# The group norm of an RWKV-7 branch: squares, sums of squares and final scaling by ScalarE's activations with bias and scale per partition

## The chip, the core and the metric

The kernel runs on one core of a Trainium2 chip. Its engines are TensorE (PE in the profile, its weight loads PEld), VectorE (DVE), ScalarE (ACT), GpSimd (POOL) and SyncE (SP), which issues nearly all DMAs. The metric is the device time of one execution in microseconds (us), lower is better.

## The reference, cut to what matters

One layer of a streaming encoder is computed for a prompt of 2048 tokens and for 8 running streams of 16 tokens each. A combined projection feeds three mixers, RWKV-7, Mamba-2 and stick-breaking attention, whose outputs go through one output projection. The part that matters here is the end of the RWKV-7 mixer, a norm over the 64 values of each head and token:

```python
def rwkv7_branch(ua, gate, S0, shift0, p):
    ...
    S_T, y = lax.scan(step, S0.astype(f32), seq)
    y = y.swapaxes(0, 1)
    mean = jnp.mean(y, axis=-1, keepdims=True)
    var = jnp.mean(jnp.square(y - mean), axis=-1, keepdims=True)
    y = (y - mean) * lax.rsqrt(var + GN_EPS) * p['rwkv_ln_w']... + p['rwkv_ln_b']...
    y = y + jnp.sum(r * k * p['rwkv_r_k'].astype(f32), axis=-1, keepdims=True) * v
    out = y.reshape(B, T, D_A) * jax.nn.silu(gate.astype(f32))
```

## The kernel before

The tokens are cut into four groups: 512 prompt tokens and all 128 sample tokens, then three times 512 prompt tokens. A group is cut into units of 256 prompt tokens, and group 0 has one more of the 128 sample tokens. The twelve RWKV heads are handled in six pairs, so that the 128 partitions hold two heads. For each pair and unit `stage_rwkv` runs `rwkv_dense` (projections of k, r, v and the gate g), `rwkv_prep` (decays, masks, products), `rwkv_inv` and `rwkv_inv2` (inverse of a triangular matrix), `rwkv_chain` (the recurrence over chunks of 64 tokens, the pass spoken of below) and `rwkv_out` (the group norm, the transpose back to channels by PE, bias, gate, and the store to the scratch tensor `oT`). The output of a unit is put off: `rwkv_out` of one unit stands in the program behind the pass of the next unit, and behind the filler work of its own step. The filler work is a list of pieces of the other mixers and of the output projection of the previous group (`fill`), spread over the twelve steps of a group.

After the RWKV and Mamba-2 stages of all groups (up to about 3060 us) comes attention with the rest of the output projection.

No instruction is issued in the order of the program text. All calls on the engines are recorded by `Plan`, which at `emit` orders them with a list scheduler: it keeps an estimate of each instruction's cost (`cost`), of the lag between engines (`LAG`) and of when a buffer comes free, and takes next the instruction that can start first; at a tie the one that stands first in the program. Every engine, SP's DMA queue too, then works through its list in that order. A tile pool's tag is a ring of buffers. Apart from two PSUM tags (`AHEAD`, pd and pg) a ring's buffers are given out strictly in the order of the program. Rings that matter here:

- `tw`: four buffers for short-lived results of all kinds (projections on their way to the token shift, the convolution, gates, squares).
- `py`: one PSUM bank, used in turn by a pass of the recurrence and by the transposed result of `rwkv_out`.
- `oo`: the output of `rwkv_out`, two buffers (one in group 0); before, the squares `ysq` too.
- `gmean`, `gvar`, `rq_m`, `rq_y`, `rq_t`: small tiles of one column per chunk, two buffers each.

In `rwkv_out` the tile `Ysb` holds a unit's y with tokens of two chunks' heads on the partitions and `m` chunks of 64 values along the free axis: m is 4 for a unit of 256 tokens and 2 for the sample unit. `small_rsqrt` takes a root's inverse on DVE: two steps to scale and guess, then three rounds of three instructions. `tw(n)` gives the next buffer of the ring, `py()` the bank, `sp` is the pool of small tiles. V, S, G and Y are VectorE, ScalarE, GpSimd and SP's queue. All engine calls pass through one helper, so the profile shows one line (L420) for all of them and is read by the names of tiles: `Ysb<-Ysb,gmean` is the subtraction, `ysq<-Ysb` the squares, `gvar<-ysq` their sum, `Ysb<-Ysb,rq_y` the scaling, `py<-ident,Ysb` the transposes, `oo<-py,vech` the copy with weight and bias.

Of the kernel before, what the change touches and what calls it, by code (L numbers as in the profile page):

```python
# [7 lines left out]
F32 = mybir.dt.float32  # L8
# [3 lines left out]
AF = mybir.ActivationFunctionType  # L12
ALU = mybir.AluOpType
AX = mybir.AxisListType
# [66 lines left out]
UN = 256  # L81
# [357 lines left out]
def _build(ctx, tc, nc, A, O):  # L439
    plan = Plan(tc)  # L440
    V, S, G, T, Y = (plan.engine(e, x) for e, x in zip("VSGTY", (nc.vector, nc.scalar, nc.gpsimd, nc.tensor, nc.sync)))
# [16 lines left out]
    def pg():  # L458
        return pp.tile([128, 512], F32, name="pg", tag="pg", bufs=3)
# [4 lines left out]
    def py():  # L464
        return pp.tile([128, 512], F32, name="py", tag="py", bufs=1)

    def mm(out, lhsT, rhs, start=True, stop=True):
        T.matmul(out, lhsT, rhs, start=start, stop=stop, skip_group_check=True)
# [17 lines left out]
    def trn(out, in_):  # L486
        k = in_.shape[0]
        T.transpose(out, in_, ident[0:k, 0:k])
# [22 lines left out]
    def small_rsqrt(ss, n, scale, eps, tag):  # L511

        m = sp.tile([128, n], F32, name="rq_m", tag=tag + "m")
        y = sp.tile([128, n], F32, name="rq_y", tag=tag + "y")
        t = sp.tile([128, n], F32, name="rq_t", tag=tag + "t")
        V.tensor_scalar(m, ss, scale, eps, ALU.mult, ALU.add)
        V.tensor_scalar(y.bitcast(I32), m.bitcast(I32), -0.5, 1597463007.0, ALU.mult, ALU.add)
        for _ in range(3):
            V.tensor_tensor(t, y, y, ALU.mult)
            V.scalar_tensor_tensor(t, t, -0.5, m, ALU.mult, ALU.mult)  # L520
            V.scalar_tensor_tensor(y, t, 1.5, y, ALU.add, ALU.mult)
        return y
# [11 lines left out]
    def tw(n):  # L534
        return wp.tile([128, 536], F32, name="tw", tag="tw", bufs=4)[:, 0:n]
# [91 lines left out]
    def h_scale(tiles, xs=None):  # L627

        n = len(tiles)
        ss = sp.tile([128, 2, 5], F32, name="hss", tag="hss")  # L630
        for i, (c, p0) in enumerate(tiles):
            for q in range(2):
                x = xs[i][q] if xs else xhalf(p0, q)
                S.activation(tw(512) if xs else x, x, AF.Square, accum_out=ss[:, q, i:i + 1])
        s1 = sp.tile([128, 5], F32, name="hs1", tag="hs1")
        V.tensor_tensor(s1[:, 0:n], ss[:, 0, 0:n], ss[:, 1, 0:n], ALU.add)
        r = small_rsqrt(s1[:, 0:n], n, 1.0 / D, 1e-6, "h")
        return [r[:, i:i + 1] for i in range(n)]
# [529 lines left out]
    def rwkv_out(g, u, d, gate, pr, Ysb, pool):  # L1168
        n, m = u.n, u.nch
        y3 = Ysb[:, 0:m, :]  # L1170
        mean = sp.tile([128, 6], F32, name="gmean", tag="gmean")
        V.reduce_sum(mean[:, 0:m], y3, axis=AX.X)
        V.tensor_scalar(mean[:, 0:m], mean[:, 0:m], 1.0 / 64, None, ALU.mult)
        V.tensor_tensor(y3, y3, mean[:, 0:m].unsqueeze(2).to_broadcast([128, m, 64]), ALU.subtract)
        sq = pool.tile([128, UN], F32, name="ysq", tag="oo", bufs=1 if g.s else 2)
        s3 = sq[:, 0:n].rearrange("p (c v) -> p c v", v=64)
        G.tensor_tensor(s3, y3, y3, ALU.mult)
        var = sp.tile([128, 6], F32, name="gvar", tag="gvar")
        V.reduce_sum(var[:, 0:m], s3, axis=AX.X)
        rs = small_rsqrt(var[:, 0:m], m, 1.0 / 64, 64e-5, "g")  # L1180
        V.tensor_tensor(y3, y3, rs.unsqueeze(2).to_broadcast([128, m, 64]), ALU.mult)
        p = py()
        if u.s:
            with plan.together():
                for c_ in range(m):
                    for o in (slice(0, 64), slice(64, 128)):
                        mm(p[o, 64 * c_:64 * c_ + 64], Ysb[o, c_, :], ident[o, o])
        else:
            for i in range(m // 2):
                trn(p[:, 128 * i:128 * i + 128], Ysb[:, 2 * i:2 * i + 2, :].rearrange("p h v -> p (h v)"))  # L1190

        o = pool.tile([128, UN], F32, name="oo", tag="oo", bufs=1 if g.s else 2)
        S.activation(o[:, :n], p[:, :n], AF.Identity, bias=vh(V_LNB + pr), scale=vh(V_LNW + pr))
        G.tensor_tensor(o[:, :n], o[:, :n], d["bo"], ALU.add)
        G.tensor_tensor(o[:, :n], o[:, :n], gate[:, u.c0:u.c0 + n], ALU.mult)
        for c, k, t in g.segs(u.c0, n):
            Y.dma_start(oT[pr, :, t:t + k], o[:, c - u.c0:c - u.c0 + k])
# [25 lines left out]
    def stage_rwkv(g, h, dpool, NB):  # L1223
# [39 lines left out]
        def chain(i):  # L1263
            pr, k = todo[i]
            uds = [(us[k], ds[pr][k])]
            S0T = None
            if k == 0 and smp:
                S0T = rwkv_states_in(pr, pool)
                uds = [(u, ds[pr][j]) for j, u in smp] + uds
            for u, d in uds:  # L1270
                prv = ds[pr][k - 1] if k and not u.s else None
                nxt = ds[pr][k + 1] if k + 1 < len(us) and not u.s else None
                y, Sn = rwkv_chain(u, d, pr, pool, S0T, prv, nxt)
                out()
                if "g" not in Ds[pr]:
                    dense(pr, "g")
                done.append(lambda u=u, d=d, y=y: rwkv_out(g, u, d, Ds[pr]["g"], pr, y, pool))
                if u.s:
                    rwkv_states_out(pr, Sn, pool)
# [269 lines left out]
    g = GROUPS[0]  # L1549
    early = ExitStack()  # L1550
    pool = early.enter_context(tc.tile_pool(name="m", bufs=1))
# [8 lines left out]
    rs = h_scale(g.tiles[:2], xt[:2])  # L1560
# [87 lines left out]
    p = pg()  # L1648
# [13 lines left out]
    def vh(i):  # L1662
        return vech[:, i:i + 1]
# [39 lines left out]
    p = pg()  # L1703
# [7 lines left out]
    p = pg()  # L1711
# [12 lines left out]
    for d in dD:  # L1724
        m = NCH * 8 * 2064 + 128
        for i in range(0, m, 128 * 323):
            n = min(128 * 323, m - i)
# [14 lines left out]
    with tc.tile_pool(name="r0", bufs=1) as pool:  # L1742
        rw.send((pool, fill))
        w = tw(512).rearrange("p (a c) -> p a c", c=128)
        p = pg()
# [16 lines left out]
    with tc.tile_pool(name="r", bufs=1) as pool:  # L1762
        for gi in range(1, len(GROUPS)):
            g = GROUPS[gi]
# [29 lines left out]
    with tc.tile_pool(name="fin", bufs=1) as pool:  # L1794
        r = pool.tile([64, 6, 128], F32, name="r")
        for q in range(2):
            p = pg()
# [7 lines left out]
        for q in range(2):  # L1805
            p = pg()
# [6 lines left out]
        p = pg()  # L1813
# [25 lines left out]
    p = pt()  # L1839
# [240 lines left out]
```

## Time and profile before

| | us |
|---|---|
| median of 3 runs | 3867.22 |
| lowest and highest run | 3865.18, 3870.82 |
| the profiled execution's own time | 3871.62 |
| its span (first to last instruction) | 3869.9 |
| PE busy | 3385.2 (87%) |
| DVE busy | 2746.8 (71%) |
| ACT busy | 1724.5 (45%) |
| POOL busy | 1672.4 (43%) |
| mean granted clock of TensorE | 0.933 |

A row of a group of instructions has the line, the engine, the operation, the tile written and, behind the arrow, the tiles read, the shapes, the count, then busy time in us and the mean duration of one in ns, and behind the second bar the idle time of the engine just before them with what ended it. A row of waits has the waiting engine and its tile, the engine and tile waited for, the us in total, the times and the longest. A row of a timeline has the start in us, the duration in us, and the instruction. Durations of neighbours on one engine overlap a little, so their sum can be more than the time they take.

### The profile page before, as it was taken

The numbers are of one execution on the slowest core, as the hardware profiler recorded it, in microseconds if no ns is written. First come the engines' busy times: TensorE is split into PE (matmuls) and PEld (weight loads), VectorE is DVE, ScalarE is ACT, GpSimd is POOL, SyncE is SP. The second block draws the span as 40 slices with busy tenths as digits, with TensorE's granted clock in tenths as the row PEclk, the third lists the DMA queues.
The fourth block names the chain that finished last, engine by engine and source line by source line (L and its number), as shares of the span: only waits on it lengthen the run. The fifth ranks groups of instructions, "written<-read, shape, count | busy, mean of one in ns | idle before, by whom it ended". The sixth has DMA issues, their size and how long they took to land. (4 is left out here: it accounts for less than half of the span.)

```text
span 3869.9 us, 68238 instructions
## 1 busy us (share of the span) xinstructions
PE 3385.2 (87%) x23086; PEld 2749.6 (71%) x23086; DVE 2746.8 (71%) x6621; ACT 1724.5 (45%) x4134; POOL 1672.4 (43%) x2621
## 2 busy tenths in 40 slices
PE   7988999977988898988889998888999688989998
PEld 7877888867776676776667777766777555666665
DVE  7657778876698778657886875688778553456665
ACT  4544444433454444434444443445444343445554
POOL 4544555434555655644456555445555323000000
PEclk9998999978989899999899999989999889999999
DMA  4332333335425433553254336324532587765542
GB/s 120 97 107 61 95 92 78 78 103 145 121 59 158 140 89 101 153 149 94 71 154 110 78 84 180 101 68 128 150 82 64 154 212 223 176 150 140 135 129 66
DMA packets 693227, 454.41 MB, mean 117 GB/s; under 512 B 259978, under 2 KB 617806, under 8 KB 692878
## 3 DMA queue, kind: packets, MB, share of 16 engines
q1 hardware_dynamic: 692878, 450.06, 43.7%
q8 instruction: 183, 3.00, 0.3%
q14 instruction: 166, 1.36, 0.1%
HBM read 362.40 MB, written 87.51 MB: 116 GB/s over the span
## 5 line engine op out<-in xcount | busy, mean ns | idle before, releaser
L420 POOL TENSOR_TENSOR wlo<-wraw,whi 128x512 fp32r<-128x512 f32 (+1 forms) x568 | 762.4, 1348 | 542.0 <-ACT whi L420 378.9
L420 ACT CAST whi<-wraw 128x512 fp32r<-128x512 f32 (+1 forms) x702 | 428.7, 620 | 407.7 <-PE pd L420 290.7
L420 PE MATMUL pd<-hh,whi 128*128 128x512 f32 (+1 forms) x1560 | 552.8, 390 | 13.6 <-ACT tw L420 10.7
L420 PE MATMUL pd<-hh,wlo 128*128 128x512 f32 (+1 forms) x1560 | 553.2, 389 | 4.4 <-POOL wlo L420 4.4
L420 PE MATMUL pd<-hl,whi 128*128 128x512 f32 (+1 forms) x1560 | 555.9, 390 | 0.0
L420 PEld LDWEIGHTS pd<-hh,whi 128*128 128x128 f32 x1560 | 296.0, 196 | 51.3 <-ACT tw L420 14.3
L420 PEld LDWEIGHTS pd<-hh,wlo 128*128 128x128 f32 x1560 | 296.3, 194 | 39.5 <-POOL wlo L420 6.4
L420 POOL TENSOR_SCALAR SE<-RV,ELl 64x64 f32<-64x64 f32 x384 | 208.1, 542 | 267.7 <-DVE RV L420 218.8
L420 PEld LDWEIGHTS pd<-hl,whi 128*128 128x128 f32 x1560 | 296.8, 195 | 34.4 <-issue 1.5
L420 PE MATMUL pd<-whi,hh 128*128 128x256 f32 (+1 forms) x1224 | 300.1, 299 | 6.2 <-DVE tw L420 3.7
L420 PE MATMUL pd<-wlo,hh 128*128 128x256 f32 (+1 forms) x1224 | 298.4, 298 | 1.3 <-POOL wlo L420 1.3
L420 PE MATMUL pd<-whi,hl 128*128 128x256 f32 (+1 forms) x1224 | 295.5, 295 | 0.2 <-DVE hl L420 0.2
L420 DVE TENSOR_TENSOR_SCAN I<-ke,I,zeros 128x512 f32<-128x512 f32 x192 | 231.8, 1266 | 82.6 <-ACT ke L420 82.6
L420 ACT COPY aT<-pt 128x512 f32<-128x512 f32 (+3 forms) x320 | 162.4, 524 | 201.8 <-PE pt L420 199.2
L420 PEld LDWEIGHTS pd<-whi,hh 128*128 128x128 f32 x1224 | 214.8, 198 | 11.4 <-DVE tw L420 4.1
L420 PE MATMUL pt<-ident,I 128*128 128x128 f32 x1088 | 180.1, 286 | 42.2 <-DVE I L420 35.9
L420 PE MATMUL zt<-kk,qt 128*128 128x512 f32 (+3 forms) x640 | 205.8, 411 | 11.7 <-DMA kk<-kS 5.7
L420 PEld LDWEIGHTS pd<-wlo,hh 128*128 128x128 f32 x1224 | 213.8, 198 | 3.0 <-POOL wlo L420 2.0
L420 PEld LDWEIGHTS pd<-whi,hl 128*128 128x128 f32 x1224 | 213.0, 198 | 1.8 <-DVE hl L420 0.4
L420 POOL TENSOR_TENSOR oc<-oc,gy 128x512 f32<-128x512 f32 x16 | 20.8, 1302 | 438.2 <-ACT aT L420 167.1
L420 DVE TENSOR_TENSOR fs<-AT,DN 32x63 f32<-32x63 f32 (+14 forms) x672 | 199.6, 297 | 12.3 <-POOL DN L420 0.5
L420 PEld LDWEIGHTS pt<-ident,I 128*128 128x128 f32 x1088 | 120.4, 143 | 115.0 <-issue 36.9
(408 smaller groups left out, 8176.7 us busy)
## 6 DMA issues: line engine op xcount, KB each, us to landing
wraw<-in_w_in SPq DMA_DIRECT2D x456, 256.0 KB
wraw<-in_w_out SPq DMA_DIRECT2D x168, 256.0 KB
kk<-kS SPq DMA_DIRECT2D x160, 256.0 KB
wraw<-oT SPq DMA_DIRECT2D x78, 256.0 KB
ab<-acS SPq DMA_DIRECT2D x34, 384.0 KB
Da<-dD SPq DMA_DIRECT2D x96, 128.0 KB
sraw<-in_x_prompt SPq DMA_DIRECT2D x48, 256.0 KB
pr<-in_w_out SPq DMA_DIRECT2D x48, 256.0 KB
```

The costliest lines, as they stand in the source:

```text
L420: r = f(*a, **k).ins
```

## The change

The mean is taken with a negative sign. The tile is no longer centred by a subtraction: for each chunk, one Square activation with the negative mean as its bias per partition writes its values into a buffer of the ring `tw` that nobody reads, and puts the sum of squares into `gvar`. The scaling is one Identity activation for each chunk, with the inverse root as scale and minus the mean times the inverse root as bias, for which one more small product is taken. GpSimd's squares, and the tile for them, are gone.

```diff
     def rwkv_out(g, u, d, gate, pr, Ysb, pool):
         n, m = u.n, u.nch
         y3 = Ysb[:, 0:m, :]
+
         mean = sp.tile([128, 6], F32, name="gmean", tag="gmean")
         V.reduce_sum(mean[:, 0:m], y3, axis=AX.X)
-        V.tensor_scalar(mean[:, 0:m], mean[:, 0:m], 1.0 / 64, None, ALU.mult)
-        V.tensor_tensor(y3, y3, mean[:, 0:m].unsqueeze(2).to_broadcast([128, m, 64]), ALU.subtract)
-        sq = pool.tile([128, UN], F32, name="ysq", tag="oo", bufs=1 if g.s else 2)
-        s3 = sq[:, 0:n].rearrange("p (c v) -> p c v", v=64)
-        G.tensor_tensor(s3, y3, y3, ALU.mult)
+        V.tensor_scalar(mean[:, 0:m], mean[:, 0:m], -1.0 / 64, None, ALU.mult)
         var = sp.tile([128, 6], F32, name="gvar", tag="gvar")
-        V.reduce_sum(var[:, 0:m], s3, axis=AX.X)
+        for i in range(m):
+            S.activation(tw(64), y3[:, i, :], AF.Square, bias=mean[:, i:i + 1], accum_out=var[:, i:i + 1])
         rs = small_rsqrt(var[:, 0:m], m, 1.0 / 64, 64e-5, "g")
-        V.tensor_tensor(y3, y3, rs.unsqueeze(2).to_broadcast([128, m, 64]), ALU.mult)
+        V.tensor_tensor(mean[:, 0:m], mean[:, 0:m], rs, ALU.mult)
+        for i in range(m):
+            S.activation(y3[:, i, :], y3[:, i, :], AF.Identity, bias=mean[:, i:i + 1], scale=rs[:, i:i + 1])
         p = py()
```

## The prediction

> **What bounds the kernel now.** I read the page's head first, then the busy time of the stretch that holds the group norm, then who TensorE (PE) waits for there, and last the rows of the norm itself.
>
> ```profile
> span 3869.9 us, 68238 instructions
> L420 DVE TENSOR_REDUCE gmean<-Ysb x54: 267/406/422, 375.3 to 3042.6; 128x4 f32<-128x256 f32 x48, 128x2 f32<-128x128 f32 x6
> ```
>
> The reader is to see that the norm runs 54 times, 48 on a tile of four 64-column chunks and 6 on a tile of two: 48 x 4 + 6 x 2 = 204 chunks, between 375 and 3043 us. What comes after is attention and can't be touched directly. Next the busy time of each engine by stretch, first the sum of four stretches that together cover 340 to 3060 us, then one token group (its first norm is at 1086 us, its twelfth at 1621) in steps of 100 us:
>
> ```profile
> core 0: us, PE busy (x) PEld busy (x) DVE busy (x) ACT busy (x) POOL busy (x), PEclk, DMA share, GB/s
> sum 2720.00, PE 2382.95 PEld 1995.38 DVE 2081.21 ACT 1165.45 POOL 1429.68; mean PE 595.74 PEld 498.85 DVE 520.30 ACT 291.36 POOL 357.42
> ...
> 1060.00:1160.00 100.00, 89.19 (x619) 71.60 (x619) 91.83 (x269) 51.31 (x133) 50.89 (x90) 0.88 0.24 58
> 1160.00:1260.00 100.00, 85.54 (x522) 66.69 (x518) 81.91 (x208) 46.50 (x112) 51.77 (x64) 0.93 0.54 156
> 1260.00:1360.00 100.00, 87.51 (x470) 70.37 (x471) 69.57 (x148) 44.62 (x104) 62.79 (x78) 0.85 0.49 138
> ...
> 1460.00:1560.00 100.00, 86.60 (x541) 64.91 (x541) 86.33 (x225) 37.68 (x98) 56.36 (x81) 0.93 0.39 107
> 1560.00:1660.00 100.00, 88.68 (x626) 79.06 (x623) 59.70 (x139) 41.82 (x96) 55.92 (x62) 0.93 0.54 156
> ...
> L420 DVE TENSOR_REDUCE gmean<-Ysb x12: 397/414/422, 1085.9 to 1621.2; 128x4 f32<-128x256 f32 x12
> ```
>
> Over the 2720 us DVE is busy 77%, POOL 53%, and ACT, which gets the work, 43%. PE's 88% flatters it, for the ends of its matmuls are modelled. In three of the seven steps DVE is above 80%, once at 92%: there its own queue sets the pace. In the others, two of them not shown, it has slack. Who ends PE's idle time (340 to 3060 us) agrees:
>
> ```profile
> engine line waited for: us in total, times, longest us
> PE pg L420 <- DVE sraw L420: 62.5, 18, 5.7
> PE pg L420 <- DVE GB L420: 36.3, 30, 3.8
> PE pz L420 <- DVE RV L420: 33.6, 36, 2.4
> PE pg L420 <- DVE BK L420: 33.3, 40, 2.6
> PE py L420 <- DVE Ysb L420: 19.6, 14, 3.1
> ...
> PE pd L420 <- ACT tw L420: 9.1, 5, 3.5
> PE py L420 <- ACT RV L420: 7.9, 19, 0.8
> PE pz L420 <- ACT ZY L420: 6.6, 11, 1.1
> ```
>
> The five largest are all DVE's, 185 us together; the three largest of ACT are 24 us. The first (sraw) is the preparation of the next group, where no norm runs.
>
> **What comes off DVE and POOL.** The subtraction, the second sum and the final product, and POOL's squares:
>
> ```profile
> L420 DVE TENSOR_TENSOR Ysb<-Ysb,gmean 128x256 f32<-128x256 f32 (+1 forms) x54 | 29.1, 540 | 1.2
> L420 DVE TENSOR_TENSOR Ysb<-Ysb,rq_y 128x256 f32<-128x256 f32 (+1 forms) x54 | 23.7, 439 | 1.2
> L420 DVE TENSOR_REDUCE gvar<-ysq 128x4 f32<-128x256 f32 (+1 forms) x54 | 21.4, 396 | 18.9 <-POOL ysq L420 18.7
> L420 DVE TENSOR_TENSOR rq_t<-rq_y 128x4 f32<-128x4 f32 x183 | 43.0, 235 | 3.7
> L420 POOL TENSOR_TENSOR ysq<-Ysb 128x256 f32<-128x256 f32 (+1 forms) x54 | 35.8, 663 | 28.9 <-DVE Ysb L420 15.5 <-DMA oT<-oo 11.3 <-DVE fs L420 1.1
> ```
>
> DVE loses 29.1 + 23.7 + 21.4 = 74.2 us and gains 54 small products (mean times rs), each like the fourth row: 54 x 0.235 = 12.7. Net 61.5 us, 3.0% of its 2081. The scale of the mean only changes sign: nothing. POOL loses 35.8 us, which I count at nothing: it is busy 53%, and no wait of PE for it is among the five. ysq also leaves the ring that it shares with oo, and with it the 11.3 us in which POOL stood still for an oT transfer; those too are POOL's and cost PE nothing.
>
> What 61.5 us of DVE are worth: the low end passes on only the share that is late, 3.0% of the 185 us: 5.5 us. The high end gives them back one for one where DVE sets the pace. Twelve norms from 1085.9 to 1621.2 us are one per 45 us or so, so the three steps above 80% hold 6.7 of 12, or 55%: 34 us. I take 18: nearer the high end than the proportion, since in 1060 to 1160 DVE leaves only 8 us idle, but only half of it, since behind each freed us stands the next DVE instruction of the recurrence or PE's answer.
>
> **What goes to ACT.** Per chunk one Square with a bias per partition, the read of its accumulator, and one Identity with bias and scale per partition, all of 64 columns. None of these sizes is in the trace; the nearest rows:
>
> ```profile
> L420 ACT ACTIVATE ab<-ab,acs 128x128 f32<-128x128 f32 x204 | 68.2, 394 | 1.0
> L420 ACT ACTIVATE sq<-sq 128x256 f32<-128x256 f32 x96 | 39.9, 416 | 1.2
> L420 ACT ACTIVATE a<-a,kahn,vech 128x256 f32<-128x256 f32 x48 | 28.7, 599 | 5.6 <-DVE ba L420 5.1
> L420 ACT ACTIVATE sq<-sq 128x128 f32<-128x128 f32 x12 | 3.7, 309 | 0.1
> ...
> 1531.49 1.28 ACT L420 ACTIVATE ab<-ab,acs 128x128 f32<-128x128 f32 x4
> ...
> 1587.69 0.19 ACT L420 ACTIVATION_READ_ACCUMULATOR tw<-ysb 128x1 f32 x1
> 1587.78 0.51 ACT L420 ACTIVATE tw<-ysb 128x384 f32<-128x384 f32 x1
> ```
>
> A column costs (416 - 309)/128 = 0.836 ns, 64 of them 53 ns. The Square with one pointer lasts 394 - 53 = 341 ns; four such instructions follow each other at (1.28 - 0.394)/3 = 0.295 us, less 0.053 is 0.242 at 64 columns. After the read the next starts 0.09 later. The Identity, with two pointers, lasts 599 - 192 x 0.836 = 438 ns, and with the same overlap of 0.10 takes 0.34. Per chunk 0.67 us, times 204: 137 us, or 12% on ACT's 1165. Cover: ACT's idle 57% in these stages. If that is gone, the next late thing is the copies of the recurrence (ZY, RV) and the casts whi that stand behind a burst of four in its queue. Low end: 12% of PE's 24 us for ACT, 3 us. High end: 12% also of the longest wait of DVE, that for ACT's tw:
>
> ```profile
> DVE tw L420 <- ACT tw L420: 118.1, 51, 13.3
> ```
>
> That is 12% of 24 + 118 = 142, so 17 us. I take 5, near the low end, because the waits of PE itself are the nearer row.
>
> New waits: rq_m, the first step of the inverse root, now waits on DVE for ACT's last accumulator read, where gvar waited 18.7 us for POOL. Everything queued on DVE stands behind it in either case: even. Squares wait for the mean, Identities for the small product; behind them in ACT's queue stand those copies and casts. No DMA is added or removed; the oT transfer of a unit keeps its place in SP's queue, and if its oo came late, the weight loads behind it would too. Square and Identity already run here between Tanh and Exp, with ten table loads in the whole span, so none is added:
>
> ```profile
> L420 ACT ACT_TABLE_LOAD x10 | 12.8, 1283 | 23.5 <-DMA kk<-kS 22.6 <-PEq L2068 0.8
> ```
>
> **The sum.** -18 + 5 = -13 us on the profiled execution's 3871.62, so 3858.6. That execution stands 4.4 above the median of the runs, 3867.22; on that footing 3854. What this kernel's timing can tell from no change I take as 0.2%, 7.7 us.
>
> **Rivals.** *DVE's freed time is filled by its own next wait.* For it: outside those three steps DVE has slack, and the largest wait (62.5) has no norm near it. Against it: 92%. It gives the low end of DVE's gain, 5.5, against ACT's 5: 3867.
>
> *ACT becomes late.* Per unit of four chunks DVE gave up (74.2 - 12.7)/54 = 1.1 us and ACT takes on 2.7, and this engine feeds the casts and the recurrence. It decides when ACT's high end is passed on while DVE's gain stays at its proportion: -5.5 + 17 = +12, so 3879. Against it: only 24 us of PE's waits are ACT's. The Trainium skill (ScalarE: Activation LUTs, section "Rules for kernel authors") says to give adds and multiplies to VectorE, which it calls up to about three times faster per element. The trace agrees on the price, since 2.7 us stand against 1.1, but the rule looks at one instruction and not at which engine is late; by it alone the sum would be 2.7 - 1.1 = 1.6 us more per unit, 86 us.
>
> *The ring of tw buffers holds the norm back* (slower). Each Square writes into its own tw, a ring of four that the planner hands out strictly in program order, and a unit's norm stands in the program behind the filler work of its step. Today the norm is free of that ring:
>
> ```profile
> 1221.92 0.42 DVE L420 TENSOR_REDUCE gmean<-Ysb 128x4 f32<-128x256 f32 x1
> 1265.15 0.57 ACT L420 ACTIVATE oo<-py,vech 128x256 f32<-128x256 f32 x1
> 1298.72 0.19 POOL L420 COPY tw<-carU 128x1 f32<-128x1 f32 x1
> ...
> 2117.34 0.22 DVE L420 TENSOR_SCALAR rq_m<-gvar 128x4 f32<-128x4 f32 x1
> 2124.87 0.43 DVE L420 TENSOR_TENSOR Ysb<-Ysb,rq_y 128x256 f32<-128x256 f32 x1
> ```
>
> This unit's mean is taken at 1221.9 and its oo at 1265.2. The last tw ahead of its place in the program is first written at 1298.7. With the Squares in between, oo comes at about 1299 + 1.3 of Squares + 8 of root (last two rows) = 1308, 43 us later, and the one py bank that it empties is what the next recurrence pass needs. For it: that order is strict. Against it: other work is there for PE meanwhile, and passes can be shortened: two means 23 us apart show one, while the average is 45.
>
> ```profile
> 1550.58 0.42 DVE L420 TENSOR_REDUCE gmean<-Ysb 128x4 f32<-128x256 f32 x1
> ...
> 1573.73 0.42 DVE L420 TENSOR_REDUCE gmean<-Ysb 128x4 f32<-128x256 f32 x1
> ```
>
> A delay decides when it is more than the 22 us that one pass can make up and the filler runs out: 43 - 22 = 21 us for one such unit in each of three groups, half of it covered by other work, is +32; less the 13, 3867 + 19 = 3886.
>
> **How the numbers follow.** The forecast has 0.53 (own range 3833, the high end of DVE's gain and no cost at ACT, to 3861); the first rival 0.24 (3860 to 3875); ACT 0.07; the ring 0.16. The planner re-plans the order of all stages with any change, so each case is spread by some us. Faster 0.53, same 0.24, slower 0.23. The range 3830 to 3886 leaves out a tail below and the upper half of the ring's case.
>
> **What would show it.** Right: DVE's busy time in 340 to 3060 us falls by some 60, ACT's rises by some 140, POOL's falls by 36; Square rows near 341 ns, reads 190, Identity near 438; the rows of PE waiting for DVE's RV, BK and GB shrink. Wrong: oo rows long after the pass that precedes them, gaps between the means of over 60 us, DVE waiting for ACT's tw by far more than 118, or PE waiting for DVE as much as before although DVE does less.

## The result, and the profile after

The changed kernel takes 3917.38 us (median; 3913.7 to 3923.34) beside 3866.2 us for the kernel before on the same chip: a ratio of 1.0139 [1.0119, 1.0158]. It is slower by 51 us, where 13 us less were forecast. Its profiled execution took 3913.7 us at a mean granted clock of 0.927.

The page's head, then the busy time summed over the same four stretches from 340 to 3060 us as before (of which the changed kernel, being late, has done a little less by then):

```profile
span 3912.0 us, 68741 instructions
PE 3419.5 (87%) x23086; PEld 2768.6 (71%) x23086; DVE 2647.8 (68%) x6513; ACT 1855.5 (47%) x4746; POOL 1626.6 (42%) x2567
...
sum 2720.00, PE 2385.77 PEld 1989.46 DVE 1953.72 ACT 1272.52 POOL 1363.05; mean PE 596.44 PEld 497.37 DVE 488.43 ACT 318.13 POOL 340.76
```

Against the table of before, over the whole span, DVE lost 99 us, POOL lost 46, ACT gained 131. So the work went where the change sends it, and the kernel still became slower. The norm's own rows (the view of one tile: shortest, median and longest in ns, first and last start in us), then the groups with their idle time:

```profile
L420 ACT ACTIVATE tw<-Ysb,gmean x204: 331/336/370, 374.7 to 3088.6; 128x64 f32<-128x64 f32 x102
L420 ACT ACTIVATION_READ_ACCUMULATOR tw<-Ysb,gmean x204: 185/187/211, 374.9 to 3088.8; 128x1 f32 x102
L420 ACT ACTIVATE Ysb<-Ysb,gmean,rq_y x204: 423/426/443, 381.9 to 3095.1; 128x64 f32<-128x64 f32 x102
L420 DVE TENSOR_REDUCE gmean<-Ysb x54: 267/406/420, 373.6 to 3085.6; 128x4 f32<-128x256 f32 x48, 128x2 f32<-128x128 f32 x6
L420 DVE TENSOR_TENSOR gmean<-gmean,rq_y x54: 142/161/1216, 381.7 to 3093.9; 128x4 f32<-128x4 f32 x48, 128x2 f32<-128x2 f32 x6
...
L420 ACT ACTIVATE tw<-Ysb,gmean 128x64 f32<-128x64 f32 x204 | 68.7, 339 | 16.2 <-DVE gmean L420 10.2 <-PE pz L420 1.4 <-DMA yS<-tw 1.3
L420 DVE TENSOR_SCALAR rq_m<-gvar 128x4 f32<-128x4 f32 (+1 forms) x54 | 15.0, 278 | 26.2 <-ACT tw L420 25.9
```

Square 336 ns, read 187, Identity 426 (forecast 341, 190, 438). DVE's wait moved from POOL's squares (18.7 us) to ACT's last accumulator (25.9). What PE waits for, 340 to 3060 us:

```profile
PE pg L420 <- DVE sraw L420: 64.6, 23, 5.9
PE pg L420 <- DVE BK L420: 36.3, 36, 2.7
PE pg L420 <- DVE GB L420: 28.9, 24, 4.3
PE pz L420 <- DVE RV L420: 21.7, 27, 2.3
PE py L420 <- ACT Ysb L420: 18.4, 15, 6.4
```

PE's waits for DVE's `RV`, `BK` and `GB` fell from 33.6 + 33.3 + 36.3 = 103.2 us to 86.9: DVE is less late, as forecast. The wait for the scaled `Ysb` (before DVE's, 19.6 us, now ACT's, 18.4) is nearly as long. None of these rows holds 50 us. What is new is only seen when one unit is followed in time. This is the unit of group 1 whose squares are held back longest of all 54, rows in order of start (start, duration, instruction, in brackets the idle time before it):

```profile
1306.78 0.41 DVE L420 TENSOR_REDUCE gmean<-Ysb 128x4 f32<-128x256 f32 x1
...
1355.15 0.33 PE L420 MATMUL py<-RV,BG 128*128 128x64 f32 x2
...
1383.69 0.39 ACT L420 ACTIVATE tw<-pd 128x256 f32<-128x256 f32 x1 [1.32 <-PE pd L420]
1384.18 0.42 DVE L420 SCALAR_TENSOR_TENSOR tw<-tw,pd 128x256 f32<-128x256 f32 x1 [1.80 <-ACT tw L420]
1384.48 0.35 ACT L420 ACTIVATE tw<-Ysb,gmean 128x64 f32<-128x64 f32 x1
...
1385.72 0.19 ACT L420 ACTIVATION_READ_ACCUMULATOR tw<-Ysb,gmean 128x1 f32 x1
1385.95 0.87 DVE L420 TENSOR_SCALAR rq_m<-gvar 128x4 f32<-128x4 f32 x1 [1.35 <-ACT tw L420]
...
1390.13 1.43 ACT L420 ACTIVATE Ysb<-Ysb,gmean,rq_y 128x64 f32<-128x64 f32 x4 [3.70 <-DVE gmean L420]
1390.95 0.14 PEld L420 LDWEIGHTS py<-ident,Ysb 128*128 128x128 f32 x1 [2.02 <-ACT Ysb L420]
...
1392.07 0.56 ACT L420 ACTIVATE oo<-py,vech 128x256 f32<-128x256 f32 x1
...
1393.48 0.33 PE L420 MATMUL py<-RV,BG 128*128 128x64 f32 x2
```

The mean is there at 1306.8, but the first Square runs at 1384.5, 78 us later and 0.8 us after a `tw` of the filler. Meanwhile the next pass has done its last product (1355.2), and its successor can't start until `oo` has emptied the `py` bank at 1392.6; it starts at 1393.5, after 38 us. In the kernel before the same unit went like this:

```profile
1268.52 0.41 DVE L420 TENSOR_REDUCE gmean<-Ysb 128x4 f32<-128x256 f32 x1
...
1272.18 0.61 POOL L420 TENSOR_TENSOR ysq<-Ysb 128x256 f32<-128x256 f32 x1 [0.36 <-DVE Ysb L420]
...
1325.59 0.43 PE L420 MATMUL py<-RV,BG 128*128 128x64 f32 x2 [0.65 <-DVE Ysb L420]
...
1327.84 0.56 ACT L420 ACTIVATE oo<-py,vech 128x256 f32<-128x256 f32 x1 [0.24 <-PE py L420]
...
1332.09 0.55 PE L420 MATMUL py<-RV,BG 128*128 128x64 f32 x4
```

There the squares follow the mean after 3.7 us, and the turn from one pass to the next takes 6 us instead of 38.

Such a gap leaves no long row of idle time: in the 38 us from 1355 to 1393 PE is busy for 32.7, with other work (gates of the Mamba-2 mixer and pieces of the output projection, in this unit). That this work then is missing when a later pass waits is a reading, not shown. Two numbers worked out from the traces measure the delay over all 54 units: from the start of a unit's mean to that of its first square 253 us in total before, 1262 after (median 3.7 and 20 us; counted to the next square of any unit, as one expectation below does, it is 1085); and from the last product of the pass that precedes an `oo` to the end of that `oo`, 227 us before, 386 after (median 3.0 and 5.6). The second is called the lateness below.

### The profile page after: what moved, and what is told of

Same layout as the page of the kernel before. It is cut to its first block, busy times and chain, and to the rows that moved or that the text cites. A ratio compares the mean times of both kernels' runs of the same rounds, so it can differ in the third digit from the quotient of the medians.

```text
span 3912.0 us, 68741 instructions
## 1 busy us (share of the span) xinstructions
PE 3419.5 (87%) x23086; PEld 2768.6 (71%) x23086; DVE 2647.8 (68%) x6513; ACT 1855.5 (47%) x4746; POOL 1626.6 (42%) x2567
## 5 line engine op out<-in xcount | busy, mean ns | idle before, releaser
L420 PE MATMUL pd<-hh,whi 128*128 128x512 f32 (+1 forms) x1560 | 567.3, 396 | 13.0 <-ACT tw L420 9.7
L420 PE MATMUL pd<-wlo,hh 128*128 128x256 f32 (+1 forms) x1224 | 306.9, 296 | 2.2 <-POOL wlo L420 2.2
L420 PE MATMUL pd<-whi,hl 128*128 128x256 f32 (+1 forms) x1224 | 306.1, 296 | 0.0
L420 DVE TENSOR_TENSOR fs<-AT,DN 32x63 f32<-32x63 f32 (+14 forms) x672 | 188.2, 280 | 11.8
```

The lines of the kernel that those rows point to most:

```text
L420: r = f(*a, **k).ins
```

## The experiments

**The ring taken away.** The Squares write into a ring of their own, nothing else is changed:

```diff
-            S.activation(tw(64), y3[:, i, :], AF.Square, ...
+            S.activation(sp.tile([128, 64], F32, name="gsq", tag="gsq"), y3[:, i, :], AF.Square, ...
```

> The changed kernel, but the Squares write into a ring of their own (two tiles of 64 columns) instead of tw. Ring theory (the Squares stand in the strict order of tw behind the filler work of their step, and so hold back the py bank and the next pass of the recurrence): the loss goes, and what is left is DVE's gain less ACT's cost, 3840 to 3862; the first Square follows the mean within some 5 us and PE's wait at the turn of two passes is back to that of before. ACT theory (137 us more on ACT delay casts and copies): stays at 3905 or above. Plan theory (any change to this planner's input costs time by a worse order, by chance): anywhere from 3850 to 3920, with Squares that follow the mean.

Measured 1.0022 [1.0002, 1.0041]. Mean to squares fell to 92 us and the lateness to 229. The Squares' row now shows a wait for the mean, 30.6 us in front of 204 instructions instead of 10.2 in the changed kernel, as it must be where they follow the mean closely:

```profile
L420 ACT ACTIVATE gsq<-Ysb,gmean 128x64 f32<-128x64 f32 x204 | 68.7, 340 | 30.8 <-DVE gmean L420 30.6
L420 ACT ACTIVATION_READ_ACCUMULATOR gsq<-Ysb,gmean 128x1 f32 x204 | 38.9, 190 | 0.0
L420 DVE TENSOR_SCALAR rq_m<-gvar 128x4 f32<-128x4 f32 (+1 forms) x54 | 15.7, 291 | 20.3 <-ACT gsq L420 19.5
```

More than a point of the 1.39 is gone with the place of these buffers. But the gain of 13 us that should now be left isn't there: the 3840 to 3862 of the ring theory were missed.

**The ring alone, in the kernel before.** POOL's squares go into `tw`:

```diff
-        sq = pool.tile([128, UN], F32, name="ysq", tag="oo", bufs=1 if g.s else 2)
+        sq = tw(UN)
```

> The kernel before, with one edit: GpSimd's squares are written into a buffer of the ring tw instead of the ring oo. No work moves to ACT, DVE and POOL do what they did. Ring theory: the squares come 20 to 70 us behind the mean as in the changed kernel, and the time rises by 25 to 60 us, to 3890 to 3925. ACT theory: no change, 3860 to 3874. Plan theory: a scatter to either side.

Measured 1.0049 [1.0031, 1.0067], 19 us and thus below the 25 to 60 that were expected, although the delays were the whole of the changed kernel's: 1235 us from mean to squares, lateness 391.

**One buffer instead of four.** All Squares of a unit share one `tw`:

```diff
+        sq = tw(UN)
...
-            S.activation(tw(64), y3[:, i, :], ...
+            S.activation(sq[:, 64 * i:64 * i + 64], y3[:, i, :], ...
```

> The changed kernel, but a unit's Squares write side by side into one buffer of tw instead of one buffer each. Place theory (it is the place in the order of tw that costs, not how many buffers a unit takes): the Squares still come some 20 us behind the mean, and the time stays at 1.0110 to 1.0160 of before. Count theory (four of four buffers per unit empty the ring, and one costs little, as GpSimd's one buffer cost 0.49%): 1.0040 to 1.0090.

Measured 1.0108 [1.0088, 1.0128], just under the place theory's range and far above the count theory's; from mean to squares 1268 us, lateness 385. At this place in the order it is the place that costs, not the number of buffers taken.

**The norm moved ahead of the filler.** Mean to Identity stand directly behind their own pass in the program, `tw` is kept:

```diff
-    def rwkv_out(g, u, d, gate, pr, Ysb, pool):
-        n, m = u.n, u.nch
+    def rwkv_norm(u, Ysb):
+        m = u.nch
...
+                rwkv_norm(u, y)
```

> The changed kernel with the same instructions and four buffers of tw per unit, but the norm (mean to Identity) is moved up in the program: directly behind the unit's own pass, ahead of the output of the unit before and of the filler work of the step. Only the transposes and what follows stay where they were. Place theory: the Squares follow the mean within some 5 us and the time falls to that of the kernel with a ring of its own, 1.0000 to 1.0050 of before. Count theory: four buffers per unit still, so 1.0090 and above.

Measured 1.0200 [1.0176, 1.0224], the slowest of all, and a clear miss of the place theory: the Squares do follow their mean (114 us in total, lateness 225, both near those with an own ring), but the time doesn't fall. It lies in the count theory's range, which this run thus doesn't exclude; a norm moved up with one buffer or with a ring of its own was not run. What the trace shows is that the other users of the ring now crowd behind the mean. Between two neighbouring means of groups 1 to 3 (33 pairs) the last quarter of the time has 0.7 first writes of a `tw` by the engines for filler, where the kernel before has 1.8 and the changed kernel 1.7; the first quarter has 3.7 against 1.7 and 2.0. The last such write stands 21.2 us ahead of the mean, against 14.3 and 15.3. And PE is idle for 522 us of this run's span, against 485 before and 493 in the changed kernel. Our reading, argued and not shown: the filler behind the Squares in the ring can't run during the pass that the Squares wait for, which is the time when PE needs it.

**ACT's load alone.** The kernel before with the 204 Squares, reads and Identities added on a constant tile, results unused:

```diff
+            S.activation(sp.tile(..., tag="gsq"), ob[:, 0:64], AF.Square, bias=mean[:, i:i + 1], accum_out=v2[:, i:i + 1])
...
+            S.activation(sp.tile(..., tag="gid"), ob[:, 0:64], AF.Identity, bias=mean[:, i:i + 1], scale=rs[:, i:i + 1])
```

> The kernel before, with the changed kernel's ACT work on top: per chunk one Square with accumulator and one Identity, both of 64 columns with the same pointers, but they read a constant tile and write tiles of their own that nobody reads, so the norm does not wait for them; they become ready when the mean and the inverse root are. It prices ACT's 137 us alone. Ring theory, with ACT's cost of the prediction: 3866 + 3 to 17, so 3869 to 3883. ACT theory: 3900 and above.

Measured 1.0037 [1.0024, 1.005]: 14 us, near the high end of 3 to 17, in one draw (see below).

**The parts of the change.** First only the final scaling on ACT; then only the squares with their sums, in an own ring; then centring and scaling by Identities, with POOL's squares and DVE's sums kept:

```diff
+            S.activation(y3[:, i, :], y3[:, i, :], AF.Identity, scale=rs[:, i:i + 1])
...
+            S.activation(sp.tile(..., tag="gsq"), y3[:, i, :], AF.Square, accum_out=var[:, i:i + 1])
...
+            S.activation(y3[:, i, :], y3[:, i, :], AF.Identity, bias=mean[:, i:i + 1])
```

> One part of the change alone: subtraction, squares and their sum as before, only the final scaling is done by ACT's Identity per chunk (scale per partition, no bias); no tw is taken. DVE loses 23.7 us, ACT gains 204 x about 0.25 us = 51. Ring theory: within 0.3% of before, 3855 to 3877. ACT theory: a good third of the loss, 3880 to 3890.

> The other part of the change alone: subtraction and scaling stay on DVE; the squares and their sum are one Square with accumulator per chunk on ACT, into a ring of their own. DVE loses 21.4 us, POOL 35.8, ACT gains 204 x about 0.3 = 61. If the parts add up (own ring +0.22%, scaling alone -0.31%): 1.0030 to 1.0080. If ACT's work has one price wherever it is put (0.37% for 137 us) and DVE's freed time the value that scaling alone shows: 0.9970 to 1.0010.

> Centring and scaling on ACT (two Identities per chunk, one pointer each), squares on GpSimd and both sums on DVE as before; no tw is taken and no accumulator read. DVE loses 29.1 + 23.7 us, ACT gains 204 x 0.5 = 100. If scaling alone is faster because DVE is freed: twice its gain, 0.9920 to 0.9970 of before. If ACT's load takes it back at 0.37% for 137 us: 0.9970 to 1.0020.

Measured 0.9969 [0.9947, 0.999], 1.0029 [1.0015, 1.0042] and 0.9950 [0.9934, 0.9966]. The first and the last came as their first theories expected; the second lies just under one of its ranges and above the other. The last beats both kernels. But the parts don't add up: scaling -0.31 and squares +0.29 don't make the +0.22 of the whole in an own ring in any way that the rows explain, and all of them are small. That raised the question how much of such a number is the order that the planner happens to write.

**The order as a draw.** One constant of the planner's estimate is moved by 2 ns; no instruction changes:

```diff
-            return half + 0.068 + n / rate + 0.06 * small
+            return half + 0.070 + n / rate + 0.06 * small      (or 0.066)
```

> The kernel before, with one constant of the planner's estimate for VectorE raised by 2 ns (0.068 to 0.070 us); no instruction is added, removed or changed, only the order that the planner writes. Theory A (the order is a draw: any edit re-plans all stages, and the parts of +-0.2 to 0.5% measured so far are partly that): the time moves by more than 0.15% in one direction or the other, 3861 or less, or 3873 or more. Theory B (the plan is stable enough that the small parts measure the engines' work): within 0.1%, 3863 to 3871.

> As the run before, with the constant lowered by 2 ns (0.068 to 0.066 us). Theory A: again more than 0.15% away from the kernel before, and not the same as with 0.070. Theory B: within 0.1%, 3863 to 3871.

> The changed kernel with the Squares in a ring of their own, and the planner's constant for VectorE at 0.070 us. Its sibling at 0.068 stood at 1.0022 of the kernel before. Theory A: another draw, anywhere from 0.997 to 1.007. Theory B: 1.0022 within 0.001. Either way it stays under 1.0095, if the ring of tw buffers is what the change pays for.

> The changed kernel with the Squares in a ring of their own and the planner's constant for VectorE at 0.066 us, without the read cost. Theory C: 0.999 to 1.004, as its siblings (1.0022, 1.0008). Theory A: anywhere from 0.994 to 1.006.

> The changed kernel itself, Squares in the ring tw, with the planner's constant for VectorE at 0.070 us. If the ring is the cause: another draw round 1.0139 and 1.0108 (the two measured with tw), from 1.007 to 1.019, above all draws with a ring of their own. If the changed kernel was an unlucky draw: below 1.005.

> The kernel before with only POOL's squares put into a buffer of the ring tw, and the planner's constant for VectorE at 0.070 us. Its sibling at 0.068 delayed the norm as much as the changed kernel does (1102 against 1085 us from means to squares) but stood at 1.0049. If the delay by the ring is the whole price (theory R): 1.007 to 1.014, and the sibling was a lucky draw. If the price needs the Squares on ACT as well, whose queue of casts stands behind them (theory Q): 1.001 to 1.007.

> As the run before with the constant at 0.066 us. Theory R: 1.007 to 1.014. Theory Q: 1.001 to 1.007.

And a repair of the estimate, which knows no accumulator read, tried with three constants:

```diff
+        accum = 0.09 if k.get("accum_out") is not None else 0.0
-        return half + (0.05 if ...
+        return half + accum + (0.05 if ...
```

> The changed kernel with the Squares in a ring of their own, and the planner told of the accumulator read: 0.09 us more for each Square that has a sum. Theory C (the rest of the loss, +0.22% where -0.3% was forecast, comes from a plan that thinks ACT's sums 0.4 us too early per unit and so sets DVE waiting): 0.997 to 0.9995 of the kernel before, 3855 to 3866. Theory A: another draw between 0.997 and 1.007, with no relation to the estimate's correctness. If ACT's 137 us themselves are the price: 1.001 to 1.004.

> Squares in a ring of their own, planner told of the accumulator read, and its constant for VectorE at 0.070 us. Theory C (the planner's missing read cost is what kept the change from paying, the size of the draw aside): 0.992 to 0.998 of the kernel before. Theory A (0.994 with the read cost was a lucky draw of an order, of a spread of about +-0.3% round the 1.0015 of the kernels with a ring of their own): more likely than not above 1.000.

> As the run before with the constant at 0.066 us. Theory C: 0.992 to 0.998. Theory A: more likely than not above 1.000.

Ratios to the kernel before (each is one draw of the order, named by the planner's constant):

| kernel | 0.068 | 0.070 | 0.066 | mean |
|---|---|---|---|---|
| before | 1 | 1.0003 [0.9988, 1.0017] | 1.0041 [1.0022, 1.0061] | 1.0015 |
| POOL's squares in `tw` | 1.0049 [1.0031, 1.0067] | 1.0055 [1.0030, 1.0080] | 1.0093 [1.0072, 1.0113] | 1.0066 |
| changed, Squares in `tw` | 1.0139 [1.0119, 1.0158] | 1.0100 [1.0072, 1.0127] | 1.0108 [1.0088, 1.0128] (one `tw`, 0.068) | 1.0116 |
| changed, own ring | 1.0022 [1.0002, 1.0041] | 1.0008 [0.9993, 1.0022] | 0.9991 [0.9975, 1.0007] | 1.0007 |
| own ring, read cost told | 0.9940 [0.9919, 0.9961] | 0.9972 [0.9956, 0.9989] | 1.0036 [1.0018, 1.0054] | 0.9983 |

Two nanoseconds in an estimate move the unchanged kernel by 0.41% in one case and by nothing in the other, so theory A held once and theory B once; the last row spreads over almost a point, its first draw under every range that was expected for it, the second in that of theory C, the third on the side of theory A. A single measured ratio within some 0.4% of another, however narrow its interval, is therefore no statement about an edit here, and by the last row even more can be the order alone. What stands above that and what doesn't, as three draws against three:

- Squares of ACT in `tw` against an own ring: all three above all three, means 1.09 points (42 us) apart. The ring's price is shown, and the changed kernel's 1.0139 is its worst draw.
- The ring with POOL's squares against the kernel before: again all above all, 1.0049 the lowest and 1.0041 the highest, 0.51 points (20 us) between the means, and 0.49 to 0.52 at each of the three constants. If narrowly, the delay alone is a price, but with the squares on ACT much the same delay costs about twice as much in these draws (of theories R and Q the draw at 0.070 fits Q, that at 0.066 R). That something in ACT's queue behind the Squares makes the difference was not shown and stays open.
- The change without the ring against the kernel before: 1.0007 against 1.0015, not to be told apart. Nor is the read cost's 0.9983, with a third draw at 1.0036, and the parts (0.9969, 1.0029, 0.9950) and ACT's load (1.0037), drawn once each, stay unsettled too. The kernel with the read cost (3847.59 us) and that with centring and scaling (3850.38 us) do beat both kernels; whether by what they compute or by their order is open.

Why the change doesn't gain without the ring can be read from what PE waits for. All its waits in 340 to 3060 us, added up by the engine waited for, as means of three draws, in us:

| | for DVE | for ACT | for all |
|---|---|---|---|
| before | 255 (240 to 267) | 43 (40 to 46) | 325 |
| changed, own ring | 225 (217 to 232) | 75 (63 to 81) | 322 |
| changed, `tw` | 228 (223 to 233) | 75 (70 to 78) | 332 |

DVE is less late, by 30 us, and ACT is later by 32. 8 to 9 us of each are the wait for the scaled `Ysb`, whose writer is now ACT; the rest shows in rows such as these, before (beside 6.6 for `ZY` and 7.9 for `RV` in the prediction) and with the own ring:

```profile
PE pd L420 <- ACT whi L420: 4.2, 8, 1.2
```

```profile
PE pz L420 <- ACT ZY L420: 14.5, 17, 1.8
PE pd L420 <- ACT whi L420: 11.7, 14, 2.0
PE py L420 <- ACT RV L420: 10.0, 18, 2.4
```

A sum of waits is not a price, but here the two sums cancel as the two kernels' times do.

Where the ring's time lies, as means over the three draws of a row, in us. A group ends at the first `dtv` of the next one, the last group at attention's first tile:

| | group 0 | group 1 | group 2 | group 3 | attention |
|---|---|---|---|---|---|
| length, changed, `tw` | 908 | 765 | 723 | 714 | 799 |
| length, own ring | 893 | 757 | 719 | 700 | 796 |
| lateness, `tw` | 129 | 104 | 72 | 83 | |
| lateness, own ring | 66 | 62 | 43 | 49 | |

Each group of the RWKV stages is longer, 41 us together, and each has its passes kept waiting longer, 168 us together: the loss is a quarter of the added lateness. With POOL's squares in `tw` it is 20 us of 143, a seventh, so the share is no constant.

How the delay becomes time is only partly seen. The spans of these profiled executions differ by 43.5 us. By the first rows of their pages, PE's idle time holds 19 of them and its busy time 24, with the same 23086 matmuls. The granted clock differs too: over all executions its mean was 0.9255 to 0.9285 in the three kernels with ACT's Squares in `tw` and 0.9309 to 0.9336 in those with an own ring; for the kernel before it was 0.933 to 0.934 from chip to chip, with 0.070 it was 0.9359, and with 0.066, the draw at 1.0041, 0.9277. In the kernel before, 0.001 less of clock goes with some 2 us more (last section). By that slope, an estimate, 10 of the 42 us go with the lower clock, and 12 of the 15 us of the draw at 1.0041. Whether an order lowers the clock or the clock moves on its own the runs don't say; between the two sets of kernels 32 us are left without it.


## Why the prediction was wrong

*The step that failed* is in the sum, -18 + 5 = -13: the delay by the ring of `tw` buffers stands in it at nothing, kept as a rival at 0.16. The runs showed +42 us for it. Its mechanism is the one that the trace shows: strict order, the norm behind the filler of its step, `oo` late, the next pass waiting for the `py` bank. Against it the prediction set "other work is there for PE meanwhile, and passes can be shortened". The first is true and no defence: PE is busy for 32.7 of the 38 us of the gap above, and the loss is there all the same. The second may be true for a part, since only a quarter of the lateness came through. That the order of a ring is strict was known from the code, so that the delay would come was certain, and only its price was in question; a chance of 0.16 treated it as if it might not come.

*The price of the ring*, +32 us from three units of 21 us, half covered: measured +42 (ACT) and +20 (POOL). The working was wrong in form, since the delay is spread over all groups, so that a sum of the right size is in part luck. 3867 + 42 - 13 would have been 3896, where 3917 was measured: the -13 wasn't there, and 1.0139 is the slowest of the draws.

*DVE's gain, -18, and ACT's price, +5.* The sum of -13 would be -0.34%. Measured without the ring: 1.0007 against 1.0015, -3 us; the differences of single draws lie between -19 and +8 us. So the draws alone neither confirm nor exclude the forecast, and the first rival (3867) fits the time as well. The waits say more: PE waits 30 us less for DVE, so by this reading the gain of DVE is there and not filled by DVE's own next wait, as that rival had it; but PE waits 32 us more for ACT. The term that was too small is ACT's: +5 was taken from 12% of PE's 24 us for ACT, as if its waits grew with its busy time, and they grew by three quarters (43 to 75). ACT's load alone showed +14, in one draw. The second rival, ACT late at 3879, has thus its mechanism in the trace, but not its time, for +12 us stands against -3. Against the Trainium skill (ScalarE: Activation LUTs, section "Rules for kernel authors"), the rule by which adds and multiplies belong on VectorE, stands that the change without the ring didn't cost the 86 us that the prediction worked out from it (by its own totals, 137 - 61.5, it would be 76): 1.0007 is 3 us. The factor of three there is given for bf16 and operations with a single source; these tiles are f32.

*The busy times* came close: ACT +131 forecast +137; POOL -46 against -36. DVE lost 99 against 61.5: the removed rows less the new product are 74.2 - 11.5 = 62.7, and the rest is that unchanged instructions were shorter on the mean in this execution (last section). With an own ring DVE lost 63 to 70.

*The rule for reading it wrong* held: "oo rows long after the pass that precedes them" is what the trace shows. "DVE waiting for ACT's tw by far more than 118" did not come (122.5). "Gaps between the means of over 60 us" says nothing: within the groups the kernel before has eight of them, the changed one seven.

*The bound for no change.* 0.2% is what a measurement tells from no change between two fixed kernels. Between two edits it is too small: another order of the unchanged kernel alone gave 0.41%.

## What to carry to other kernels

Before an operation gets a scratch output, look at whose ring the buffer comes from and where the operation stands in that ring's order: a result that nobody reads cost 42 us here because its buffer stood in line behind other stages' work. Before work moves to an idler engine, look at what the critical engine waits for there: these waits grew by three quarters (43 to 75 us) while ACT's busy time in those stages was forecast to grow by 12%. And where a scheduler re-plans everything, time an edit over several harmless perturbations of the plan before believing a few tenths of a per cent.

## What the runs showed of the hardware

The time of one and the same kernel follows the granted clock of the execution. Over 25 executions of the kernel before on one chip the fastest, 3859.32 us, had 0.940, the slowest, 3882.21 us, had 0.929, and the correlation is -0.90; which is the cause of the other the runs don't say.

A mean can hide that most instructions didn't change. Rows of DVE before, then after, of an instruction that the edit doesn't touch (behind the first bar busy us and mean ns):

```profile
L420 DVE SCALAR_TENSOR_TENSOR rq_t<-rq_t,rq_m 128x4 f32<-128x4 f32 (+4 forms) x309 | 82.4, 267 | 7.3
```

```profile
L420 DVE SCALAR_TENSOR_TENSOR rq_t<-rq_t,rq_m 128x4 f32<-128x4 f32 (+4 forms) x309 | 75.2, 245 | 6.5
```

The median is 163 ns before and 161 after. The mean is made by a tenth of them that last over 600 ns, mostly about 1.2 us: 10.4% before, 8.7% after. It isn't the removed work that does it: with an own ring, where the same work is removed, the mean is 248 to 260 ns in three draws; with POOL's squares in `tw`, where none is, 232 to 260; with the norm moved ahead 299. The page's busy time of an engine holds these long ones, so a fall of 99 us isn't 99 us of removed work. What makes them long was not tried.
